# Weight sums of the next pair in another buffer, GpSimd operations in pieces, gate rows asked one item ahead, in one decoder layer

## The chip, the cores and the metric

The kernel runs on one core of a Trainium2 chip. The metric is the device time of one execution in microseconds (us), as the median of several executions. The engines are named as in the profile: PE is TensorE (PEld its weight loads), DVE is VectorE, ACT is ScalarE, POOL is GpSimd, SP is SyncE, which here issues most DMA transfers.

## The reference

One layer of a hybrid decoder on 1024 positions and 16 learned meta tokens (1040 rows of 1024 channels), all in float32: a short gated convolution and stick-breaking attention in parallel on one normalised input, merged by sigmoid gates, then a gated MLP with a causal convolution.

```python
def hybrid_mixer(xn, w_in, conv_w_mix, w_proj_conv, w_proj_attn, b_gate, w_out):
    h = xn @ w_in
    b_c, c_c, h_c, q, k, v, g_conv, g_attn = jnp.split(h, list(splits), axis=-1)
    y_conv = b_c * causal_dwconv(c_c * h_c, conv_w_mix)
    branch_conv = y_conv @ w_proj_conv
    o = stick_breaking_attention(q.reshape(hd), k.reshape(hd), v.reshape(hd))
    branch_attn = o.reshape(bsz, seq_len, D_ATTN) @ w_proj_attn
    merged = sigmoid(g_conv + b_gate[0]) * branch_conv + sigmoid(g_attn + b_gate[1]) * branch_attn
    return merged @ w_out

def conv_gated_mlp(xn, w_up_gate, conv_w_ffn, w_down):
    u, g = jnp.split(xn @ w_up_gate, 2, axis=-1)
    u = causal_dwconv(u, conv_w_ffn)
    return (jax.nn.gelu(u) * g) @ w_down
```

In the attention a weight is A[t,s] = sigmoid(z_ts) times the product over s < j < t of (1 - sigmoid(z_tj)), for s < t. Around each sub-layer stand RMS norms: x plus the norm of the mixer's result, and that plus the norm of the MLP's result.

## The kernel before

All products are made in a three-product form of reduced float32: each operand is split into a high part (a cast, `hi`) and a low part (the operand less its high part, `lo`), and PE adds hi x hi, hi x lo and lo x hi. `split(hi, lo, src, engine)` is that step: ACT casts (L64), then DVE or POOL subtracts (L65). The three matmul lines of a dense chunk are L128 to L130; the weights of a chunk are cast by ACT (L109) and split by POOL in four pieces (`wlo`, L112).

The work runs in stages. After the input norm (0 to 50 us) come the columns of `w_in` in chunks of 342 rows, interleaved with the attention (to about 1000 us): for each head and block of queries PE makes `z`, ACT the sigmoids, DVE scans from the right (`fl`, L340), POOL multiplies (`be`, L343) and cuts off the upper triangle (L344), and PE transposes the weights (L377), which DVE splits (`al`, L65). The helper around the kernel lays out the order of instructions on each engine by a planner, so a change of buffers or of code order can move rows elsewhere too.

Then, from about 1000 to 1220 us, the two branch projections follow, in items of 128 output channels. `item_pc(ob)` multiplies the convolution branch by its gate rows (`gcl`) and stores the product in `m_d`. `item_pa(ob)` loads the attention gate's rows (`gal`, L612) and the stored branch (`ml`, L613), DVE multiplies the projection by the gate (L615), POOL adds `ml` (L616) in three chunks, the first two query blocks are split into `mb`, and the rest goes to `mm_d` (L625). Between these items SP loads the rows of `w_out` (L640), ACT casts them and POOL splits them (`w_o`, L65). The loads share a few rotating buffers (`raw`, `gal`).

From 1220 to 1335 us nine row blocks of 114 rows go through the output projection. Each has two norms: the sum over the squares, `rstd_of` (L72 to L77, small DVE operations with a square root on ACT), the row plus the input (`row`, L732), its squares, a second `rstd_of`, and the normalised row `xv` (L738). `xvs` are two buffers for the input row and the normalised row, by turns, so the last block (8) uses `xvs[0]`. PE transposes `xv` (L745) into `xr`, and the operations `x_t1` to `x_t4` (L775) and `op_split` make from it the operands of a Strassen-Winograd product (`opB`, `opT`).

From 1335 to 1790 us 22 pairs of weight blocks are multiplied, seven products each (L863, L865, L867). `prep_pair` makes the seven weight operands of a pair: A11, S1, S2, A12, S3, S4, A22. S1 is the sum of two quarter blocks, made in `tmp_s` (L835), S2, S3 and S4 are differences in `raw` (L775), and `keep` splits each into an `a_op` buffer, cast on ACT and difference on POOL. When A22 is split, the next pair's load takes its `raw` buffer. ACT copies three partial results of a product to `snap` (L872, L875, L878). The pair's preparation runs while the pair before is multiplied, and pair 1's begins during the last row norms. The down projection fills the rest.

Of the kernel before, what the change touches and what calls it, by code (L numbers as in the profile page):

```python
# [11 lines left out]
ALU = mybir.AluOpType  # L12
# [20 lines left out]
def block_kernel(ctx, tc, x, meta_tokens, g_pre_mix, w_in, channels, w_proj_conv,  # L33
# [25 lines left out]
    act_d = tc.dram_tile([DFF, D], F32, name="act_d")  # L59
    h_d = tc.dram_tile([NQ, D], F32, name="h_d")  # L60


    def split(hi, lo, src, lo_engine=None):
        nc.scalar.copy(hi, src)  # L64
# [250 lines left out]
    def stage1(p, h, g):  # L315
# [3 lines left out]
        for b in range(3 * g, 3 * g + 3):  # L319
# [19 lines left out]
            def weights(fl=fl, be=be, nk=nk):  # L339
                nc.vector.tensor_tensor_scan(fl[:, :nk][:, ::-1], fl[:, :nk][:, ::-1],  # L340
                                             upper[:, NT - nk:][:, ::-1], 1.0,
                                             op0=ALU.mult, op1=ALU.max)
                nc.gpsimd.tensor_tensor(be[:, 0:nk - 1], be[:, 0:nk - 1], fl[:, 1:nk], op=ALU.mult)  # L343
                nc.gpsimd.affine_select(out=be[:, nk - QB:nk], in_=be[:, nk - QB:nk],  # L344
                                        pattern=[[-1, QB]], compare_op=ALU.is_gt, fill=0.0,
                                        base=0, channel_multiplier=1)
                pad = min(P * (-(-nk // P)), nk_end)
                if pad > nk:
                    nc.gpsimd.memset(be[:, nk:pad], 0.0)
# [229 lines left out]
    def src_of(tiles):  # L579
# [3 lines left out]
            return t[:, 0, kb, o:o + n], t[:, 1, kb, o:o + n]  # L583
        return src

    def item_pc(ob):
        st = {}

        def evac(ci, a, n, ps):
            if ci == 0:  # L590
                st["g"] = sw.tile([P, NT], F32, name="gcl", tag="wk")
                nc.sync.dma_start(st["g"][:, :NQ], gc_d[ob * P:(ob + 1) * P, :])
            g = st["g"]
            nc.vector.tensor_tensor(g[:, a:a + n], g[:, a:a + n], ps, op=ALU.mult)
            if ci == 2:
                nc.sync.dma_start(m_d[ob * P:(ob + 1) * P, :], g[:, :NQ])
        return (col_block(w_proj_conv, ob), src_of(yT), CH3, evac)
# [5 lines left out]
        return mb[b]  # L603

    def item_pa(ob):
        st = {}

        def evac(ci, a, n, ps):
            if ci == 0:
                st["g"] = sw.tile([P, NT], F32, name="gal", tag="wk")  # L610
                st["m"] = sw.tile([P, NT], F32, name="ml", tag="ld")
                nc.sync.dma_start(st["g"][:, :NQ], ga_d[ob * P:(ob + 1) * P, :])  # L612
                nc.sync.dma_start(st["m"][:, :NQ], m_d[ob * P:(ob + 1) * P, :])  # L613
            g, m = st["g"][:, a:a + n], st["m"][:, a:a + n]
            nc.vector.tensor_tensor(g, g, ps, op=ALU.mult)  # L615
            nc.gpsimd.tensor_tensor(g, g, m, op=ALU.add)  # L616
            if ci == 0:
                for b in range(2):
                    t = mb.get(b)
                    if t is None:  # L620
                        t = m_tile(b)
                    split(t[:, 0, ob, :], t[:, 1, ob, :], g[:, b * QB:(b + 1) * QB])
            if ci == 2:
                gv = st["g"][:, 2 * QB:NQ].rearrange("p (b n) -> p b n", n=QB)
                nc.sync.dma_start(mm_d[:, :, ob * QB:(ob + 1) * QB].rearrange("b p n -> p b n"), gv)  # L625
        return (col_block(w_proj_attn, ob), src_of(oT), CH3, evac)

# [62 lines left out]
    def load_m(b):  # L690
# [3 lines left out]
        raw = raw.rearrange("p (k n) -> p k n", k=KB)  # L694
        nc.sync.dma_start(raw, mm_d[b - 2].rearrange("p (k n) -> p k n", k=KB))
        t = m_tile(b)
        split(t[:, 0], t[:, 1], raw, nc.gpsimd if b > 5 else nc.vector)

    def out_products(b, c):
        n = min(CH, D - c * CH)  # L700
# [115 lines left out]
    def prep_pair(i):  # L816
# [7 lines left out]
        else:  # L824
            tmp_s = shared.get("tmp")
            if tmp_s is None:
                tmp_s = shared["tmp"] = mpool.tile([P, 512], F32, name="tmp_s", tag="mb")

        def keep(name, src):
            t = ring_tile()  # L830
            split(t[:, 0], t[:, 1], src, nc.gpsimd)
            got[name] = t

        keep("A11", a11)
# [400 lines left out]
```

## Time and profile before

| what | value |
|---|---|
| median of 3 runs | 2044.26 us (2043.37 to 2045.91) |
| profiled execution, its own time | 2045.85 us |
| its span | 2044.2 us |
| mean granted clock of PE | 0.993 |
| DMA | 177.58 MB, 87 GB/s on average |
| POOL instructions | 998 |

The span is the stretch that the trace covers, 1.65 us shorter than the execution. Durations of single instructions and waits come from this one execution. A row such as "PE tp L745 <- DVE xv L738" says that PE's `tp` instructions of line 745 waited for DVE's `xv` of line 738. The granted clock is PE's clock as a share of full speed.

### The profile page before, as it was taken

Reading aid. Unit: us, or ns where it says so; the run is one execution under the profiler, and the core shown is the slowest. Engines: PE = TensorE matmul, PEld = TensorE weight load, DVE = VectorE, ACT = ScalarE, POOL = GpSimd, SP = SyncE. Lnnn points to the kernel's source line nnn. Section 1 sums busy time; section 2 is a strip of 40 time slices with the busy share of each in tenths; the row PEclk is TensorE's granted clock in tenths of the full one; section 3 lists DMA queues with packets and bytes.
Section 4 is the critical chain, followed back from the end, with each engine's and each line's share of the span. In section 5 each row is a group of like instructions: output and inputs, shape, how many; then the busy total and the mean of one; then the engine's idle time right before and its main releaser. Section 6 shows DMA issues by size and latency. Waiting matters only on the chain.

```text
span 2044.2 us, 30953 instructions
## 1 busy us (share of the span) xinstructions
PE 1982.2 (97%) x12228; PEld 1857.7 (91%) x12228; DVE 1006.6 (49%) x1545; ACT 851.5 (42%) x1771; POOL 997.5 (49%) x998
## 2 busy tenths in 40 slices
PE   6999999999999999999999989979999999999997
PEld 6999999999999999999999989968998898878886
DVE  6545555555555555553341115784444434445546
ACT  5544555555554545554421113453344344421122
POOL 2543666465555646564223550336565555654353
PEclk9999999999999999999999999989999999999999
DMA  3111101111111111012574664313221212253223
GB/s 136 42 63 42 53 31 65 41 52 42 45 50 42 62 38 56 32 62 74 175 228 157 184 184 120 103 44 99 88 83 62 104 63 83 73 176 119 88 83 134
DMA packets 56174, 177.58 MB, mean 87 GB/s; under 512 B 12872, under 2 KB 12872, under 8 KB 56028
## 3 DMA queue, kind: packets, MB, share of 16 engines
q1 hardware_dynamic: 52704, 165.09, 24.9%
q10 hardware_dynamic: 3324, 10.50, 1.7%
q8 instruction: 96, 1.57, 0.3%
q14 instruction: 50, 0.41, 0.1%
HBM read 131.36 MB, written 44.21 MB: 86 GB/s over the span
## 4 chain that ended last, share of the span: by engine, by line
PE 79%; DVE 8%; DMA 6%; ACT 3%; POOL 2%; issue 2%; ACTq 0%; DVEq 0%; SPq 0%; POOLq 0%
PE mm L128 13%; PE mm L129 13%; PE mm L130 13%; PE st L863 6%; PE st L867 6%; PE st L865 6%; PE tp L377 3%; PE st L1155 3%; PE st L1157 3%; PE st L1156 3%; PE av L367 2%; PE av L368 2%; DMA xv<-in_x_dram 2%; PE z L331 2%; PE z L330 2%
## 5 line engine op out<-in xcount | busy, mean ns | idle before, releaser
L128 PE MATMUL mm<-xnT,whi 128*128 128x342 f32 (+2 forms) x1536 | 506.1, 330 | 0.3 <-ACT xnT L64 0.2
L129 PE MATMUL mm<-xnT,whi 128*128 128x342 f32 (+2 forms) x1536 | 493.5, 321 | 0.5 <-DVE xnT L65 0.5
L130 PE MATMUL mm<-xnT,wlo 128*128 128x342 f32 (+2 forms) x1536 | 492.0, 320 | 0.0
L112 POOL TENSOR_TENSOR wlo<-raw,whi 128x256 fp32r<-128x256 f32 x320 | 270.0, 876 | 208.0 <-ACT whi L109 207.9
L343 POOL TENSOR_TENSOR be<-be,fl 114x127 f32<-114x127 f32 (+2 forms) x144 | 181.0, 1257 | 284.0 <-DVE fl L340 268.0
L128 PEld LDWEIGHTS mm<-xnT,whi 128*128 128x128 f32 x1536 | 289.6, 189 | 5.0 <-ACT xnT L64 0.8
L129 PEld LDWEIGHTS mm<-xnT,whi 128*128 128x128 f32 x1536 | 290.2, 189 | 2.1 <-DVE xnT L65 1.0
L130 PEld LDWEIGHTS mm<-xnT,wlo 128*128 128x128 f32 x1536 | 289.7, 189 | 0.0
L340 DVE TENSOR_TENSOR_SCAN fl<-fl,upper 114x128 f32<-114x128 f32 (+2 forms) x144 | 215.6, 1499 | 117.0 <-ACT fl L332 103.0
L65 POOL TENSOR_TENSOR a_op<-raw,a_op 128x512 fp32r<-128x512 f32 (+1 forms) x136 | 191.2, 1419 | 91.4 <-ACT a_op L64 88.8
L65 DVE TENSOR_TENSOR al<-tp,ah 128x342 fp32r<-128x342 f32 (+4 forms) x288 | 127.1, 450 | 147.3 <-ACT ah L64 146.0
L64 ACT CAST ah<-tp 128x342 fp32r<-128x342 f32 (+4 forms) x288 | 112.8, 398 | 168.5 <-PE tp L377 160.2
L863 PE MATMUL st<-opT,a_op 128*128 128x258 f32 (+2 forms) x528 | 171.9, 326 | 4.7 <-ACT snap L878 1.6
L865 PE MATMUL st<-opT,a_op 128*128 128x258 f32 (+2 forms) x528 | 169.7, 321 | 2.9 <-DVE opT L65 2.0
L867 PE MATMUL st<-opT,a_op 128*128 128x258 f32 (+2 forms) x528 | 169.4, 321 | 0.0
L332 ACT ACTIVATE fl<-z 114x348 f32<-114x348 f32 (+10 forms) x240 | 111.5, 465 | 128.8 <-PE z L331 121.7
L64 ACT CAST a_op<-raw 128x512 fp32r<-128x512 f32 (+1 forms) x136 | 85.0, 634 | 154.7 <-DMA raw<-in_w_up_gate_dram 51.7
L1162 DVE TENSOR_TENSOR acc<-acc,st 128x512 f32<-128x512 f32 x144 | 98.5, 687 | 91.1 <-PE st L1157 91.1
L863 PE MATMUL st<-opB,a_op 128*128 128x512 f32 (+2 forms) x396 | 127.5, 322 | 0.0
L865 PE MATMUL st<-opB,a_op 128*128 128x512 f32 (+2 forms) x396 | 127.5, 322 | 0.0
L867 PE MATMUL st<-opB,a_op 128*128 128x512 f32 (+2 forms) x396 | 127.1, 321 | 0.0
L377 PE MATMUL tp<-ident,be 114*128 114x114 f32 x720 | 119.0, 263 | 6.8 <-DVE al L65 5.8
(169 smaller groups left out, 4314.0 us busy)
## 6 DMA issues: line engine op xcount, KB each, us to landing
raw<-in_w_in_dram SPq DMA_DIRECT2D x64, 512.0 KB, 3.4
raw<-in_w_up_gate_dram SPq DMA_DIRECT2D x44, 512.0 KB, 3.4
act_d<-owork SPq DMA_DIRECT2D x22, 512.0 KB, 4.3
araw<-act_d SPq DMA_DIRECT2D x22, 512.0 KB
raw<-in_w_down_dram SPq DMA_DIRECT2D x22, 512.0 KB, 3.4
y_d<-yy SPq DMA_DIRECT2D x8, 513.0 KB
ga_d<-gt SPq DMA_DIRECT2D x8, 513.0 KB
o_d<-ot SPq DMA_DIRECT2D x8, 513.0 KB
```

The source lines that it names most:

```text
L64: nc.scalar.copy(hi, src)
L65: (lo_engine or nc.vector).tensor_tensor(lo, src, hi.bitcast(F32), op=ALU.subtract)
L112: nc.gpsimd.tensor_tensor(lo[:, c], raw[:, c], hi[:, c].bitcast(F32), op=ALU.subtract)
L128: nc.tensor.matmul(ps, wh, xh, start=(kb == 0), stop=False)
L129: nc.tensor.matmul(ps, wh, xl, start=False, stop=False)
L130: nc.tensor.matmul(ps, wl, xh, start=False, stop=(kb == KB - 1))
L340: nc.vector.tensor_tensor_scan(fl[:, :nk][:, ::-1], fl[:, :nk][:, ::-1], upper[:, NT - nk:][:, ::-1], 1.0, op0=ALU.mult, op1=ALU.max)
L343: nc.gpsimd.tensor_tensor(be[:, 0:nk - 1], be[:, 0:nk - 1], fl[:, 1:nk], op=ALU.mult)
L377: nc.tensor.transpose(tp[:n, QB * j:QB * (j + 1)], blocks[j][0][:, kb * P:kb * P + n], ident[:QB, :QB])
L863: nc.tensor.matmul(ps, wt[:, 0, k], xh, start=start and kb == 0, stop=False, skip_group_check=True)
L865: nc.tensor.matmul(ps, wt[:, 0, k], xl, start=False, stop=False, skip_group_check=True)
L867: nc.tensor.matmul(ps, wt[:, 1, k], xh, start=False, stop=stop and kb == 3, skip_group_check=True)
```

## The change

There are three parts. The buffer `tmp_s` for the sums of pairs 1 and later is no longer a tile of the pool of `mb` but the first half of `xvs[0]`. POOL's operations are cut: the beta product (`be`) into pieces of at most 384 columns, the weight operands (`keep`, now by `pool_split`) into two of 256, the splits of the row blocks 6 to 8 (`mb`) into four of 228, the cast with them. And `fetch` asks for the gate rows of the next item (with `ml` in the attention projection) at the second chunk of the item before.

```diff
--- before.py
+++ after.py
@@ -59,6 +59,13 @@
     act_d = tc.dram_tile([DFF, D], F32, name="act_d")
     h_d = tc.dram_tile([NQ, D], F32, name="h_d")
 
+
+    def pool_split(hi, lo, src, pieces):
+        nc.scalar.copy(hi, src)
+        w = src.shape[-1] // pieces
+        for k in range(pieces):
+            c = slice(k * w, (k + 1) * w)
+            nc.gpsimd.tensor_tensor(lo[:, c], src[:, c], hi[:, c].bitcast(F32), op=ALU.subtract)
 
     def split(hi, lo, src, lo_engine=None):
         nc.scalar.copy(hi, src)
@@ -340,7 +347,11 @@
                 nc.vector.tensor_tensor_scan(fl[:, :nk][:, ::-1], fl[:, :nk][:, ::-1],
                                              upper[:, NT - nk:][:, ::-1], 1.0,
                                              op0=ALU.mult, op1=ALU.max)
-                nc.gpsimd.tensor_tensor(be[:, 0:nk - 1], be[:, 0:nk - 1], fl[:, 1:nk], op=ALU.mult)
+                w = -(-(nk - 1) // (-(-nk // 384)))
+                for a in range(0, nk - 1, w):
+                    e = min(a + w, nk - 1)
+                    nc.gpsimd.tensor_tensor(be[:, a:e], be[:, a:e], fl[:, a + 1:e + 1],
+                                            op=ALU.mult)
                 nc.gpsimd.affine_select(out=be[:, nk - QB:nk], in_=be[:, nk - QB:nk],
                                         pattern=[[-1, QB]], compare_op=ALU.is_gt, fill=0.0,
                                         base=0, channel_multiplier=1)
@@ -583,14 +594,25 @@
             return t[:, 0, kb, o:o + n], t[:, 1, kb, o:o + n]
         return src
 
+    fetched = {}
+
+    def fetch(kind, ob):
+        if ob > 7 or (kind, ob) in fetched:
+            return
+        g = sw.tile([P, NT], F32, name=f"g{kind}l", tag="wk")
+        nc.sync.dma_start(g[:, :NQ], (gc_d if kind == "c" else ga_d)[ob * P:(ob + 1) * P, :])
+        m = None
+        if kind == "a":
+            m = sw.tile([P, NT], F32, name="ml", tag="ld")
+            nc.sync.dma_start(m[:, :NQ], m_d[ob * P:(ob + 1) * P, :])
+        fetched[kind, ob] = (g, m)
+
     def item_pc(ob):
-        st = {}
-
         def evac(ci, a, n, ps):
-            if ci == 0:
-                st["g"] = sw.tile([P, NT], F32, name="gcl", tag="wk")
-                nc.sync.dma_start(st["g"][:, :NQ], gc_d[ob * P:(ob + 1) * P, :])
-            g = st["g"]
+            fetch("c", ob)
+            g = fetched["c", ob][0]
+            if ci == 1:
+                fetch("c", ob + 1)
             nc.vector.tensor_tensor(g[:, a:a + n], g[:, a:a + n], ps, op=ALU.mult)
             if ci == 2:
                 nc.sync.dma_start(m_d[ob * P:(ob + 1) * P, :], g[:, :NQ])
@@ -603,15 +625,12 @@
         return mb[b]
 
     def item_pa(ob):
-        st = {}
-
         def evac(ci, a, n, ps):
-            if ci == 0:
-                st["g"] = sw.tile([P, NT], F32, name="gal", tag="wk")
-                st["m"] = sw.tile([P, NT], F32, name="ml", tag="ld")
-                nc.sync.dma_start(st["g"][:, :NQ], ga_d[ob * P:(ob + 1) * P, :])
-                nc.sync.dma_start(st["m"][:, :NQ], m_d[ob * P:(ob + 1) * P, :])
-            g, m = st["g"][:, a:a + n], st["m"][:, a:a + n]
+            fetch("a", ob)
+            gt, mt = fetched["a", ob]
+            if ci == 1:
+                fetch("a", ob + 1)
+            g, m = gt[:, a:a + n], mt[:, a:a + n]
             nc.vector.tensor_tensor(g, g, ps, op=ALU.mult)
             nc.gpsimd.tensor_tensor(g, g, m, op=ALU.add)
             if ci == 0:
@@ -621,7 +640,7 @@
                         t = m_tile(b)
                     split(t[:, 0, ob, :], t[:, 1, ob, :], g[:, b * QB:(b + 1) * QB])
             if ci == 2:
-                gv = st["g"][:, 2 * QB:NQ].rearrange("p (b n) -> p b n", n=QB)
+                gv = gt[:, 2 * QB:NQ].rearrange("p (b n) -> p b n", n=QB)
                 nc.sync.dma_start(mm_d[:, :, ob * QB:(ob + 1) * QB].rearrange("b p n -> p b n"), gv)
         return (col_block(w_proj_attn, ob), src_of(oT), CH3, evac)
 
@@ -694,7 +713,11 @@
         raw = raw.rearrange("p (k n) -> p k n", k=KB)
         nc.sync.dma_start(raw, mm_d[b - 2].rearrange("p (k n) -> p k n", k=KB))
         t = m_tile(b)
-        split(t[:, 0], t[:, 1], raw, nc.gpsimd if b > 5 else nc.vector)
+        if b > 5:
+            for k in range(0, KB, 2):
+                split(t[:, 0, k:k + 2], t[:, 1, k:k + 2], raw[:, k:k + 2], nc.gpsimd)
+        else:
+            split(t[:, 0], t[:, 1], raw)
 
     def out_products(b, c):
         n = min(CH, D - c * CH)
@@ -824,11 +847,11 @@
         else:
             tmp_s = shared.get("tmp")
             if tmp_s is None:
-                tmp_s = shared["tmp"] = mpool.tile([P, 512], F32, name="tmp_s", tag="mb")
+                tmp_s = shared["tmp"] = xvs[0][:, :512]
 
         def keep(name, src):
             t = ring_tile()
-            split(t[:, 0], t[:, 1], src, nc.gpsimd)
+            pool_split(t[:, 0], t[:, 1], src, 2)
             got[name] = t
 
         keep("A11", a11)
```

What becomes of this in the order of instructions, at three places. First SP in the middle of the attention projection. The rows are the store of an item, the load of rows of `w_out` (into `raw`), the load of the stored branch (`ml`), of the attention gate's rows (`gal`) and of the next item's projection weights. Before:

```order
L625 DMA mm_d<-gal 128x7x114
L640 DMA raw<-in_w_out_dram 128x1024
L613 DMA ml<-m_d 128x1026
L612 DMA gal<-ga_d 128x1026
L100 DMA raw<-in_w_proj_attn_dram 128x1024
```

After:

```order
L644 DMA mm_d<-gal 128x7x114
L607 DMA ml<-m_d 128x1026
L659 DMA raw<-in_w_out_dram 128x1024
L603 DMA gal<-ga_d 128x1026
L107 DMA raw<-in_w_proj_attn_dram 128x1024
```

Only `ml` has moved, ahead of the load of `w_out`; `gal` keeps its place, and so do the gate rows `gcl` of the convolution projection.

Next POOL in the same stage: the additions of an item (`gal<-gal,ml`), the split of `w_out` (`w_o`) and of the next weights (`wlo`). Before:

```order
L65 TENSOR_TENSOR w_o<-raw,w_o 128x8x128
L616 TENSOR_TENSOR gal<-gal,ml 128x342 x2
L112 TENSOR_TENSOR wlo<-raw,whi 128x256 x4
L616 TENSOR_TENSOR gal<-gal,ml 128x342
L65 TENSOR_TENSOR w_o<-raw,w_o 128x8x128
```

After:

```order
L72 TENSOR_TENSOR w_o<-raw,w_o 128x8x128
L635 TENSOR_TENSOR gal<-gal,ml 128x342
L119 TENSOR_TENSOR wlo<-raw,whi 128x256 x4
L635 TENSOR_TENSOR gal<-gal,ml 128x342 x2
L72 TENSOR_TENSOR w_o<-raw,w_o 128x8x128
```

One addition has moved from behind the split of `w_out` to ahead of it.

Last DVE in the last row norm and behind it, up to the operands of pair 0 and the sums of pair 1. Before, the norm:

```order
L72 TENSOR_SCALAR v<-s_14221 114x1
L757 COPY xr<-tp 128x4x114
L74 RECIPROCAL s<-s 114x1
L835 TENSOR_TENSOR tmp_s<-raw 128x512
L75 SCALAR_TENSOR_TENSOR t<-s,v 114x1
L775 TENSOR_TENSOR raw<-raw 128x512
L76 TENSOR_SCALAR t<-t 114x1
L775 TENSOR_TENSOR raw<-tmp_s,raw 128x512
L77 TENSOR_TENSOR s<-s,t 114x1
L732 SCALAR_TENSOR_TENSOR row_13092<-row_13092,s,xv_13090 114x1024
L72 TENSOR_SCALAR v<-s_14235 114x1
L74 RECIPROCAL s<-s 114x1
```

After, the norm:

```order
L81 RECIPROCAL s<-s 114x1
L82 SCALAR_TENSOR_TENSOR t<-s,v 114x1
L83 TENSOR_SCALAR t<-t 114x1
L84 TENSOR_TENSOR s<-s,t 114x1
L755 SCALAR_TENSOR_TENSOR row_13236<-row_13236,s,xv_13234 114x1024
L79 TENSOR_SCALAR v<-s_14403 114x1
L81 RECIPROCAL s<-s 114x1
L82 SCALAR_TENSOR_TENSOR t<-s,v 114x1
L83 TENSOR_SCALAR t<-t 114x1
```

The operations `tmp_s<-raw`, `raw<-raw` and `raw<-tmp_s,raw` have left it. They now stand further on, after the norm's transposes, among the operands of pair 0 (`opB`, `opT`; `xv` is the buffer that took the place of `tmp_s`):

```order
L72 TENSOR_TENSOR opB_14380<-xr,opB_14380 128x4x256
L72 TENSOR_TENSOR opT_13225<-xr,opT_13225 128x4x115
L858 TENSOR_TENSOR xv_13234<-raw 128x512
L798 TENSOR_TENSOR xr<-xr 128x1024
L798 TENSOR_TENSOR raw<-raw 128x512
L798 TENSOR_TENSOR xr<-xr 128x1024
L72 TENSOR_TENSOR opT_14381<-xr,opT_14381 128x4x256
L798 TENSOR_TENSOR xr<-xr 128x1024
L72 TENSOR_TENSOR opT_14379<-xr,opT_14379 128x4x256
L941 TENSOR_TENSOR owork<-st,snap 128x255
L72 TENSOR_TENSOR opT_14470<-xr,opT_14470 128x4x256
L798 TENSOR_TENSOR raw<-xv_13234,raw 128x512
```

The last of the three stands behind the split of the last operand, `opT_14470`.

## The prediction

> **What bounds the kernel now.** I read the page's engine shares and chain first, then TensorE's waits, then the stretches in which those waits fall, then the timelines of the engines that end them. From the page:
>
> ```profile
> PE 1982.2 (97%) x12228; PEld 1857.7 (91%) x12228; DVE 1006.6 (49%) x1545; ACT 851.5 (42%) x1771; POOL 997.5 (49%) x998
> PE 79%; DVE 8%; DMA 6%; ACT 3%; POOL 2%; issue 2%; ACTq 0%; DVEq 0%; SPq 0%; POOLq 0%
> ```
>
> TensorE (PE) is busy 97% of the span and holds 79% of the chain that ends last; GpSimd (POOL) works 49%. An added POOL instruction therefore costs only where PE waits for what stands behind it, and the change can win no more than PE's waits and the slow clock that follows them. PE's waits in the whole program (us in all, times, longest one):
>
> ```profile
> PE tp L745 <- DVE xv L738: 7.6, 2, 6.8
> PE mm L128 <- DVE gal L615: 7.0, 1, 7.0
> PE tp L377 <- DVE al L65: 5.8, 8, 2.0
> PE st L865 <- DVE opT L65: 2.0, 2, 1.7
> PE st L863 <- ACT snap L878: 1.6, 2, 1.3
> ```
>
> The first, 6.8 of its 7.6 us in one piece, is the norm of the last row block; the second, one wait of 7.0 us, lies at the end of the attention projection; the third, eight waits of up to 2.0, is the attention's transposes; the last two are the operands and weight sums of the first pairs. The three parts of the change point at these rows. Around them the clock falls (length, busy PE, PEld, DVE, ACT, POOL with counts, then the granted clock, the DMA share, GB/s):
>
> ```profile
> 1205.65:1212.47 6.82, 4.25 (x15) 4.25 (x16) 1.73 (x5) 1.28 (x5) 5.18 (x6) 0.50 0.70 219
> 1335.00:1350.00 15.00, 8.05 (x46) 7.87 (x47) 12.02 (x25) 7.03 (x10) 1.24 (x1) 0.66 0.10 31
> 1350.00:1375.00 25.00, 21.30 (x120) 18.36 (x119) 23.30 (x19) 15.87 (x24) 12.48 (x8) 0.93 0.13 43
> ```
>
> At half clock the 4.25 us of work in the first row cost half of that, 2.1 us, beside the wait of 7.0 us. The waits and the slow clock of these rows are the largest that the change reaches, so the result is decided at about 1200 and between 1335 and 1380 us.
>
> **The change, step by step.** POOL's timeline in the middle of the attention projection and at its end serves two of the steps (start, length, line, tiles, count, and in brackets the wait before):
>
> ```profile
> 1154.60 2.22 POOL L65 TENSOR_TENSOR w_o<-raw,w_o 128x1024 fp32r<-128x1024 f32 x1 [6.68 <-ACT w_o L64]
> 1156.78 1.81 POOL L616 TENSOR_TENSOR gal<-gal,ml 128x342 f32<-128x342 f32 x2
> 1158.54 2.82 POOL L112 TENSOR_TENSOR wlo<-raw,whi 128x256 fp32r<-128x256 f32 x4
> ...
> 1168.84 2.21 POOL L65 TENSOR_TENSOR w_o<-raw,w_o 128x1024 fp32r<-128x1024 f32 x1 [6.59 <-ACT w_o L64]
> ...
> 1203.89 2.18 POOL L65 TENSOR_TENSOR w_o<-raw,w_o 128x1024 fp32r<-128x1024 f32 x1 [4.35 <-ACT w_o L64]
> 1206.02 0.91 POOL L616 TENSOR_TENSOR gal<-gal,ml 128x342 f32<-128x342 f32 x1
> ```
>
> *Pieces in stage 1.* POOL works off four tiles of 256 columns in 2.82 us and one of 1024 in 2.18 to 2.22, so a cut costs (2.82 - 2.18) / 3 = 0.21 us. The beta product (`be`) by shape, and POOL's wait for it:
>
> ```profile
> L343 POOL TENSOR_TENSOR be<-be,fl 114x1039 f32<-114x1039 f32 x16 | 32.5, 2030 | 4.4 <-DVE fl L340 3.9
> ```
>
> ```profile
> POOL be L343 <- DVE fl L340: 268.0, 64, 7.8
> ```
>
> The beta product of 1039 columns takes 2030 ns; in three pieces 2.03 + 2 x 0.21 = 2.45 us. The change adds 144 such instructions, 144 x 0.21 = 30 us of POOL, in stages where POOL sits idle 268.0 us before this very product: the idle time covers it. What can be won is a part of the 5.8 us in which PE waits for DVE's `al`, if DVE's scan no longer stands behind a whole product; the ends are -3 (half of the eight waits) and +1 (the affine select comes 0.42 us later in the long blocks, and one wait in three takes it over). I take -0.5, near zero, because the releaser is DVE's own split and not POOL.
>
> *Attention projection.* POOL's order changes: of an item's three additions (gate product plus convolution branch) one now stands behind the split of w_out (`w_o`), where two stood. SP's changes too: the branch rows `ml` are asked ahead of the w_out load. The gate rows `gal` keep their place behind it. SP's timeline in the middle of the stage, before the change:
>
> ```profile
> 1147.06 0.33 SPq L640 DMA_DIRECT2D raw<-in_w_out_dram  x1
> 1147.44 0.42 SPq L613 DMA_DIRECT2D ml<-m_d  x1
> 1152.74 0.32 SPq L612 DMA_DIRECT2D gal<-ga_d  x1
> ```
>
> POOL is in a ring here: the w_out split ends at 1156.82, two additions (1.8) and four splits of the next projection weights (2.8) follow, then the next w_out load is asked, lands, is cast and split. One addition fewer ahead of the weights shortens a turn by 0.9 us. Against that, `ml`, 128 x 1026 x 4 bytes, goes into the same queue ahead of w_out's 128 x 1024 x 4. How much it delays w_out no row shows. The lower end is nothing (w_out is asked 4 to 5 us after the store and `ml` may be through by then), the upper end is one whole transfer of that size, which these rows of the chain of waits give:
>
> ```profile
> 1152.74 3.49 DMA gal<-ga_d
> ...
> 1187.29 4.36 DMA raw<-in_w_out_dram
> ...
> 1195.02 7.72 DMA raw<-in_w_out_dram
> ...
> 1370.47 3.40 DMA raw<-in_w_up_gate_dram
> ```
>
> So a turn of 14.24 us (1154.60 to 1168.84) becomes 0.9 shorter to 2.6 longer (3.49 - 0.9). I take half a transfer less the addition, 1.75 - 0.9 = +0.85 us, for the turns in which both meet, and these are few, since POOL's ring only reaches PE at its end. There the order is unchanged: four splits, the w_out load (1195.02, landed 7.72 us later), the split at 1203.89, the addition at 1206.02, then this on VectorE (DVE):
>
> ```profile
> 1207.66 1.35 DVE L615 TENSOR_TENSOR gal<-gal,mm 128x342 f32<-128x342 f32 x3
> ```
>
> Nothing of that chain is taken out. The load took 7.72 us where the one before it took 4.36: with 4.36 again the chain ends 3.4 us sooner whatever the change does, with `ml` in its way it does not. Ends for this term: all of the wait and its slow clock down to the 2 us that the other stretches keep, (7.0 - 2) + 2.1 = -7; six turns at about +1 that reach PE, +6. I take -0.5: the end of the chain a little earlier by one addition, the transfer as long as it was.
>
> *The last row norm.* Three DVE operations of pair 1 (the sum `tmp_s` and two differences `raw`) leave the chain of the row norm; the DVE timeline has them in it:
>
> ```profile
> 1335.69 0.67 DVE L835 TENSOR_TENSOR tmp_s<-raw 128x512 f32<-128x512 f32 x1
> 1336.45 0.69 DVE L775 TENSOR_TENSOR raw<-raw 128x512 f32<-128x512 f32 x1
> 1337.25 0.69 DVE L775 TENSOR_TENSOR raw<-tmp_s,raw 128x512 f32<-128x512 f32 x1
> 1338.05 1.28 DVE L732 SCALAR_TENSOR_TENSOR row<-row,s,xv 114x1024 f32<-114x1024 f32 x1
> ...
> 1362.78 1.21 DVE L65 TENSOR_TENSOR opT<-xr,opT 128x1024 fp32r<-128x1024 f32 x1
> ...
> 1373.90 0.69 DVE L835 TENSOR_TENSOR tmp_s<-raw 128x512 f32<-128x512 f32 x1 [1.05 <-DMA raw<-in_w_up_gate_dram]
> 1374.68 1.70 DVE L775 TENSOR_TENSOR raw<-raw 128x512 f32<-128x512 f32 x1
> 1376.48 1.61 DVE L775 TENSOR_TENSOR raw<-tmp_s,raw 128x512 f32<-128x512 f32 x1
> ```
>
> Each puts off the next link of the norm by about 0.6 us less what the small operations hide of one another; they take 0.67 + 0.69 + 0.69 = 2.05, of which I count 1.6 (lower end 1.2, upper end 2.05). In rows 5 to 7 the product with the gain (`row<-po`) moves ahead of one operation on the transposed rows; that can bring the later row norms forward by nothing or by one such operation (1.28 from the row above is the nearest of that size); I take 1.0. So this term is -2.6, and the last opT split (1362.78) comes that much earlier, at about 1360.2, ending 1361.4.
>
> *Pair 1's sums, now behind that split.* The three operations do not vanish. The S2 difference now stands behind the last opT split, so its cast and its split on POOL start at 1361.4 + 0.69 = 1362.1 or later. POOL and ScalarE (ACT) at this place:
>
> ```profile
> 1366.65 3.80 POOL L65 TENSOR_TENSOR a_op<-raw,a_op 128x512 fp32r<-128x512 f32 x2 [1.52 <-ACT a_op L64]
> ```
>
> ```profile
> 1378.65 0.58 ACT L878 COPY snap<-st 128x512 f32<-128x512 f32 x1
> ```
>
> Behind S2 on POOL come S3, S4 and A22. One a_op split took 1.90 us here (3.80 for two), and a cut adds 0.21: four times 2.11 is 8.4, so A22 is done at 1362.1 + 0.6 for S2's cast + 8.4 = 1371.1, where the load of pair 2 that waits for it was asked at 1370.47. That load (3.40 us) leads to pair 2's three sums (from 1373.90), to the cast of its S2, and behind that cast stands ACT's copy `snap` (1378.65), for which PE waits (the row of L863 among its waits). So PE, which comes 2.6 us sooner, waits 1.3 + 2.6 us and more at that copy: the whole gain is given back. What softens it are the two differences at 1374.68 and 1376.48, 1.70 and 1.61 us beside running POOL splits where they take 0.69 alone: shorter pieces let them start earlier, by up to 2 x 0.95 = 1.9 us. The ends: 0 (A22 2 us earlier and both differences short) and +5 (A22 1.5 us later, the clock halved once more). I take +2.6, exactly what the norm won.
>
> The clock belongs to this term. The row of 1350 to 1375 us shows 0.93, that is (1 - 0.93) x 25 / 0.5 = 3.5 us at half clock, though PE's longest wait there is the 1.7 us of L865. So short waits already cost a slow stretch here, and the new, longer wait takes the place of one rather than adding one: 0. The Trainium skill ("TensorE: Matmul & The Clock Gate", Part 1) puts the halving after an idle window of some 3.4 us; by that rule the present stretch would have no slow clock and the new wait of 4 us would bring one, an estimate of +1.7 us and a sum of +0.2 in place of -1.5. The 0.93 does not agree with it as it stands.
>
> *Pieces in the products.* 22 pairs x 7 splits = 154 cuts at 0.21 us, 32 us of POOL. DVE waits for these splits, DVE's differences are long beside them, and PE waits little (the third fence, 1400 to 1800 us, where products and their sums meet):
>
> ```profile
> DVE raw L775 <- POOL a_op L65: 106.6, 20, 7.6
> ```
>
> ```profile
> L775 DVE TENSOR_TENSOR raw<-raw 128x512 f32<-128x512 f32 x39 | 48.7, 1249 | 107.5 <-POOL a_op L65 106.6
> ```
>
> ```profile
> PE st L863 <- ACT snap L872: 0.6, 2, 0.4
> PE st L863 <- DVE owork L918: 0.6, 1, 0.6
> ```
>
> The differences take 1249 ns on average where 0.69 is the bare time, and DVE idles 106.6 us before them; but PE's own two waits there are 1.2 together. The ends are -1.2 and +1 (32 us more on an engine which half the time waits for something else); I take -0.5. The nine cuts of the `mb` splits lie before the rows that need them and are in the -2.6.
>
> The sum: -0.5 - 0.5 - 2.6 + 2.6 - 0.5 = -1.5 us against the profiled execution, whose own time was 2045.85 (span 2044.2 and 1.65 around it): 2044.35. That execution stood 1.59 over the median of the runs shown, 2044.26, so the forecast for the median is 2042.8. What a measurement of this kernel can tell from no change is about 0.2%, 4.1 us: I forecast no difference.
>
> **The rivals.** *Faster: POOL's ring opens.* If `ml` has landed before w_out is asked, each turn is 0.9 us shorter, the last load is asked sooner and takes 4.36 as the one before it; the split ends 3.4 + 0.9 earlier, PE's wait falls from 7.0 to under 3, its slow clock goes, -7 as above, with half of the row norm's gain kept: -8.5, some 2036. For it: the shorter order, and that 4.36 was the usual length. Against it: the last turn's order is the same. *Slower: `ml` ahead of w_out.* At each turn w_out lands later by what of `ml` is still under way. It decides from 0.9 us on, where the addition saved is used up; at one whole transfer, 3.49, a turn is 2.6 longer. PE needs this only as far as its lead over POOL is used up, which at 1200 it is: three turns at 2.2 give +6.5, some 2051. For it: the last load shows that the queue can take 7.72, and PE has no lead left at 1200. Against it: `ml` in the second place had been in the queue as well, right behind. *Slower too: the wait at the copy grows.* If the eight pieces behind S2 meet the 128 x 1024 operations of DVE one after the other, A22 ends 3 us later than reckoned, PE waits near 7 us at the copy and some 2 us of slow clock follow: 5 more than forecast, 2047.8. *The change does not do what it says:* the gate rows `gal` still stand behind w_out and still wait for a buffer, so only `ml` moves, by one place; then the second term is 0 and the time 2043.3, inside the forecast.
>
> **How the numbers follow.** The forecast, with the rival that nothing moves, 0.43, by itself 2040.2 to 2047.5; the open ring 0.34, 2033 to 2040; `ml` in the way 0.17 and the grown wait 0.06, 2047.5 to 2053. The forecast and the nearer halves of both sides make 2034 to 2051, outside which the rest of about 0.2 lies. Faster by more than 0.2%: 0.34; within: 0.43; slower: 0.23.
>
> **What would show it.** The first step is right if the waits of L377's counterpart stay between 3 and 6 us. The second: SP's timeline shows w_out landing later after its issue or not, and TensorE's wait for `gal` near 1200 is again 5 to 8 us (the open ring: under 3). The third: no sum of pair 1 between the links of the norm, and the wait for `xv` near 5 instead of 6.8 us. The fourth: PE's wait for the third `snap` near 1376 grows from 1.3 to 3 to 6 us, and the load of pair 2 is asked at 1370 to 1372. The fifth: the differences at 0.7 to 1.0 us on average, with no change of PE's time from 1400 to 1790. The prediction is wrong first of all if the transfers in the projection stage fall out otherwise than before, and next if pair 2's load comes as early as the row norm gained.

## The result and the profile after

The changed kernel takes 2074.35 us (median of 4 runs, 2072.27 to 2078.19) against 2044.57 for the kernel before: the ratio is 1.0154, with a 95% interval from 1.0138 to 1.0169. It is 1.5%, some 30 us, slower, where no difference was forecast.

The engines' shares on the page of the changed kernel:

```profile
PE 1992.7 (96%) x12228; PEld 1864.7 (90%) x12228; DVE 997.5 (48%) x1545; ACT 852.9 (41%) x1780; POOL 1066.1 (51%) x1305
```

POOL has 307 instructions and 68.6 us more than before (1066.1 against 997.5); the prediction's count of cuts, 0.21 us each, gave 64. The loss does not lie in that sum but in where PE waits and in the slow clock behind some of these waits. PE's waits in the whole changed kernel (us in all, times, longest):

```profile
PE st L886 <- ACT snap L895: 16.4, 9, 1.9
...
PE st L886 <- ACT snap L901: 7.1, 2, 6.1
PE tp L768 <- DVE xv L761: 5.4, 2, 5.2
PE st L886 <- DVE owork L941: 5.1, 8, 1.0
PE mm L135 <- DVE gal L634: 4.8, 3, 3.8
PE tp L388 <- DVE al L72: 4.5, 8, 2.1
```

Three of the waits of before have shrunk: `xv` from 6.8 to 5.2 us at the longest, and in all `gal` from 7.0 to 4.8 and `al` from 5.8 to 4.5. For `xv` and `al` that holds in every profiled kernel of this document with the same part of the change. For `gal` it does not: in the nine kernels with the old loads of the gate rows the wait is 2.6 to 7.0 us, in the seven with the new ones 4.3 to 8.7. Two rows are new in size. The copy of L901 (L878 before), behind pair 2's casts, grew from 1.6 to 7.1. And the first copy of a product, L895 (L872 before), now holds PE nine times for 16.4 us, 1.7 to 1.9 each; before it had 0.6 in the products. Where these lie, by the same stretch of the products in both kernels, first before and then after (length, busy PE, PEld, DVE, ACT, POOL, then clock, DMA share, GB/s):

```profile
1400.00:1800.00 400.00, 396.98 (x2461) 354.06 (x2460) 178.78 (x216) 166.49 (x285) 228.98 (x167) 1.00 0.24 85
```

```profile
1400.00:1800.00 400.00, 380.20 (x2366) 340.42 (x2366) 162.72 (x203) 157.03 (x274) 244.75 (x291) 0.99 0.22 72
```

PE is idle 3 us of 400 before and 20 after, at a clock of 1.00 and 0.99. If the n-th matmul of one trace is held against the n-th of the other, the changed kernel is 0.1 us ahead at 1180 us of before, 0.8 ahead at 1213 and 5.5 ahead at 1364; between 1374 and 1387 it loses 7.0; from 1394, where it is 1.7 behind, to 1773 it falls back evenly to 28.9 behind; to the end nothing more happens (29.0). So some 27 us were lost, nearly evenly, over the products of pairs 2 to 21, a stretch to which the prediction had given -0.5. Over the same matmuls, again before and after:

```profile
1394.04:1790.08 396.04, 394.52 (x2476) 353.52 (x2474) 176.55 (x214) 164.95 (x283) 225.89 (x166) 1.00 0.23 80
```

```profile
1395.70:1819.13 423.43, 402.89 (x2475) 359.07 (x2474) 175.19 (x216) 165.01 (x283) 257.38 (x298) 0.99 0.23 74
```

Of the 27.4 us, 19.0 are idle time of PE (20.5 us against 1.5). The other 8.4 are longer work of PE (402.9 against 394.5); three stretches of 3.4 us at half clock account for 5.1 of these, and the rest is not explained here.

**How the even loss comes about.** In every second pair POOL also multiplies three results (`owork<-owork,snap`) between the weight splits of the next pair. POOL's timeline there, before:

```profile
1418.77 3.80 POOL L65 TENSOR_TENSOR a_op<-raw,a_op 128x512 fp32r<-128x512 f32 x3 [2.08 <-ACT a_op L64]
1423.80 1.31 POOL L931 TENSOR_TENSOR owork<-owork,snap 128x512 f32<-128x512 f32 x1 [1.23 <-DVE snap L930]
1425.07 1.30 POOL L65 TENSOR_TENSOR a_op<-raw,a_op 128x512 fp32r<-128x512 f32 x1
1426.33 1.30 POOL L931 TENSOR_TENSOR owork<-owork,snap 128x512 f32<-128x512 f32 x1
1427.59 1.29 POOL L65 TENSOR_TENSOR a_op<-raw,a_op 128x512 fp32r<-128x512 f32 x1
1428.84 1.31 POOL L931 TENSOR_TENSOR owork<-owork,snap 128x512 f32<-128x512 f32 x1
1430.48 1.29 POOL L65 TENSOR_TENSOR a_op<-raw,a_op 128x512 fp32r<-128x512 f32 x1 [0.33 <-ACT a_op L64]
```

and after:

```profile
1421.71 3.53 POOL L68 TENSOR_TENSOR a_op<-raw,a_op 128x256 fp32r<-128x256 f32 x5 [1.28 <-ACT a_op L64]
1426.48 1.31 POOL L954 TENSOR_TENSOR owork<-owork,snap 128x512 f32<-128x512 f32 x1 [1.23 <-DVE snap L953]
1427.75 1.44 POOL L68 TENSOR_TENSOR a_op<-raw,a_op 128x256 fp32r<-128x256 f32 x2
1429.14 1.31 POOL L954 TENSOR_TENSOR owork<-owork,snap 128x512 f32<-128x512 f32 x1
1430.41 1.44 POOL L68 TENSOR_TENSOR a_op<-raw,a_op 128x256 fp32r<-128x256 f32 x2
1431.82 1.31 POOL L954 TENSOR_TENSOR owork<-owork,snap 128x512 f32<-128x512 f32 x1
1433.09 0.73 POOL L68 TENSOR_TENSOR a_op<-raw,a_op 128x256 fp32r<-128x256 f32 x1
```

Before, three whole splits stand ahead of the first multiplication (S2, A12, S3), S4 ahead of the second, A22 ahead of the third. After, there are five pieces ahead of the first, and between the multiplications two pieces each time, which are no longer one operand: S3's second with S4's first, then S4's second with A22's first, and A22's second behind the third. Counted from the first instruction behind the first multiplication (1425.07 before, 1427.75 after), S4 is done 1.3 us later in the kernel before and 3.4 us later in the changed one, A22 3.8 and 6.1 us later. Each of the two is the last reader of a buffer into which half of the next pair's weights are loaded. SP's issue of the first of these loads, before and after:

```profile
1426.39 0.33 SPq L813 DMA_DIRECT2D raw<-in_w_up_gate_dram  x1
```

```profile
1431.18 0.33 SPq L836 DMA_DIRECT2D raw<-in_w_up_gate_dram  x1
```

It goes out at the end of S4's split in both. (The second load waits for A22's split.) ACT then waits for it, with the cast of the next pair's A11, and the copy on which PE depends stands behind that cast. ACT before, ACT after, and PE after:

```profile
1429.78 0.62 ACT L64 CAST a_op<-raw 128x512 fp32r<-128x512 f32 x1 [3.98 <-DMA raw<-in_w_up_gate_dram]
1430.31 0.37 ACT L872 COPY snap<-st 128x258 f32<-128x258 f32 x1
```

```profile
1434.59 0.62 ACT L64 CAST a_op<-raw 128x512 fp32r<-128x512 f32 x1 [5.57 <-DMA raw<-in_w_up_gate_dram]
1435.11 0.37 ACT L895 COPY snap<-st 128x258 f32<-128x258 f32 x1
```

```profile
1435.53 0.39 PE L886 MATMUL st<-opT,a_op 128*128 128x258 f32 x1 [1.82 <-ACT snap L895]
```

Before, the copy is done at 1430.68 and the same matmul starts at 1430.73 without a wait; after, PE waits 1.82 us in the shown place (2.1 from the start of one matmul to the start of the next). Since the next loads wait for the next splits, the delay comes again in every second pair.

### The profile page after: what moved, and what is told of

Its sections match the earlier page's. It is cut to its first block, busy times and chain, and to the rows that moved or that the text cites. A ratio compares the mean times of both kernels' runs of the same rounds, so it can differ in the third digit from the quotient of the medians.

```text
span 2072.7 us, 31226 instructions
## 1 busy us (share of the span) xinstructions
PE 1992.7 (96%) x12228; PEld 1864.7 (90%) x12228; DVE 997.5 (48%) x1545; ACT 852.9 (41%) x1780; POOL 1066.1 (51%) x1305
## 3 DMA queue, kind: packets, MB, share of 16 engines
q1 hardware_dynamic: 52704, 165.09, 24.9%
## 5 line engine op out<-in xcount | busy, mean ns | idle before, releaser
L353 POOL TENSOR_TENSOR be<-be,fl 114x271 f32<-114x271 f32 (+14 forms) x288 | 206.0, 736 | 261.7 <-DVE fl L347 254.2
L68 POOL TENSOR_TENSOR a_op<-raw,a_op 128x256 fp32r<-128x256 f32 x264 | 214.2, 837 | 68.3 <-ACT a_op L64 65.0
L886 PE MATMUL st<-opT,a_op 128*128 128x258 f32 (+2 forms) x528 | 174.5, 330 | 28.6 <-ACT snap L895 16.4
L64 ACT CAST a_op<-raw 128x512 fp32r<-128x512 f32 x132 | 80.9, 621 | 175.4 <-DMA raw<-in_w_up_gate_dram 75.8
L886 PEld LDWEIGHTS st<-opT,a_op 128*128 128x128 f32 x528 | 101.0, 191 | 44.6 <-ACT snap L895 18.5
L888 PE MATMUL st<-opB,a_op 128*128 128x512 f32 (+2 forms) x396 | 129.1, 326 | 2.0 <-DVE opB L72 1.9
L886 PE MATMUL st<-opB,a_op 128*128 128x512 f32 (+2 forms) x396 | 129.0, 326 | 0.0
L890 PE MATMUL st<-opB,a_op 128*128 128x512 f32 (+2 forms) x396 | 128.5, 324 | 0.0
```

Source lines behind the costliest of these rows:

```text
L68: nc.gpsimd.tensor_tensor(lo[:, c], src[:, c], hi[:, c].bitcast(F32), op=ALU.subtract)
L353: nc.gpsimd.tensor_tensor(be[:, a:e], be[:, a:e], fl[:, a + 1:e + 1], op=ALU.mult)
L886: nc.tensor.matmul(ps, wt[:, 0, k], xh, start=start and kb == 0, stop=False, skip_group_check=True)
L888: nc.tensor.matmul(ps, wt[:, 0, k], xl, start=False, stop=False, skip_group_check=True)
L890: nc.tensor.matmul(ps, wt[:, 1, k], xh, start=False, stop=stop and kb == 3, skip_group_check=True)
```

## The experiments

Theory A is this one: the place of the second pieces of S4 and A22 costs the time. Theory B gives it to the cuts' own price, theory C to the other parts of the change. Each run was timed beside the kernel before, whose median was 2042.7 to 2046.4 us in these sessions; ratios and differences are to the kernel before in the same session, while the expected times were reckoned from about 2044. Where a stretch of a trace is given, it comes from one profiled execution of each kernel.

**Whole operands, cuts alone, cuts in the old order, whole operands in a late place.** The first changes one line of the changed kernel, as shown; the second puts the cut operands alone into the kernel before:

```diff
-            pool_split(t[:, 0], t[:, 1], src, 2)
+            split(t[:, 0], t[:, 1], src, nc.gpsimd)
```

> The changed kernel with the weight operands split whole again (128x512), all else as changed. Theory A (the place): cut in two, the second pieces of S3, S4 and A22 stand one multiplication `owork<-owork,snap` later on POOL, so the buffers of the next pair's weights come free 2.1 us later, ACT's cast of A11 waits for them, and the copy `snap` behind it holds PE 2 us in every second pair; whole operands restore the order, so the time falls by about 28 us to 2042 to 2048. Theory B (the price): each cut costs 0.21 us on POOL, 1.5 us a pair, and that lengthens every pair; the same fall. Theory C (the other parts: the sums in xvs[0], the beta pieces, the fetch): the time stays at 2070 to 2078.

> The kernel before with the weight operands cut in two and nothing else. Theories A and B: 2069 to 2077, PE's wait of 2 us for the first snap copy in every second pair. Theory C: 2042 to 2047.

Measured: whole operands 2047.79 us, ratio to before 1.0007 (0.9995 to 1.0018); cuts alone 2074.04 us, 1.0136 (1.0119 to 1.0154). The cut of the weight operands is the whole loss, and the other parts together win nothing that can be told. Theory C falls; A and B are not told apart.

The third keeps all cuts and binds POOL's order, for which it also starts the preparation of a pair two steps earlier; the fourth cuts nothing and binds S4 and A22 behind one more multiplication (the main lines of both edits):

```diff
+ # third, on the changed kernel: each multiplication behind the last piece placed before it
+                with tc.issue_after(last_cut[0].ins):
+                    nc.gpsimd.tensor_tensor(v, v, s, op=ALU.mult)
+ # fourth, on the kernel before
+            if name in ("S4", "A22") and i > 1 and i % 2 == 0:
+                with tc.issue_after(mults[-2 if name == "S4" else -1].ins):
+                    split(t[:, 0], t[:, 1], src, nc.gpsimd)
```

> The changed kernel with all its cuts, but POOL's order bound so that both pieces of S3 stand ahead of the first multiplication, both of S4 ahead of the second and both of A22 ahead of the third, as the whole ones did before. Theory A: S4 is done 0.14 us later than whole and A22 0.28, so most of the 28 us comes back: 2043 to 2050, the wait for the first snap copy under 0.5 us. Theory B: the cuts are all there, so 2068 to 2076.

> The kernel before, no cut anywhere, but in every second pair S4's split is put behind the second multiplication on POOL and A22's behind the third: each 1.31 us later. Theory A: the first load of the next pair comes 1.3 us later, less some 0.25 us of slack, ten times: 2052 to 2058, with PE waits of about 1 us at the first snap copy. Theory B: no cut, no cost, 2042 to 2047.

Measured: cuts in order 2050.32 us, 1.0019 (1.0008 to 1.0029); late whole operands 2064.95 us, 1.0090 (1.0073 to 1.0108), 18.6 us over before. Theory B is refuted twice: with all 154 cuts the loss is 4 us, and with none at all it is 18.6. (The third alone would not do it, as the earlier preparation is a second difference.) The late place's price was larger than the 8 to 14 expected. PE's waits in the third and in the fourth kernel:

```profile
PE st L889 <- ACT snap L904: 10.8, 11, 6.4
```

```profile
PE st L867 <- ACT snap L876: 15.6, 10, 3.1
...
PE st L867 <- DVE owork L922: 4.6, 8, 1.2
```

The fourth has the waits of the changed kernel without a cut: the first copy (L876) ten times, and a second kind, for DVE's `owork`. In the third the first copy's row has shrunk to a single wait of 0.8 us; the 10.8 us at the third copy (L904) are 6.4 once at pair 2, 1.0 once before it and, over the products, nine short waits of 0.4 at most, where ACT now has two casts ahead of that copy instead of one.

**ACT's cast behind the copy.** The changed kernel, with A11's cast bound behind the latest copy:

```diff
+            if i > 1 and name == "A11":
+                with tc.issue_after(last_snap[0].ins):
+                    pool_split(t[:, 0], t[:, 1], src, 2)
```

> The changed kernel, all cuts and POOL's order as in it, but ACT's cast of A11 is bound behind the latest `snap` copy, so that the late load of the next pair no longer stands between PE and that copy. Theory A, by this path (late split, late load, ACT's cast waits, the copy behind it waits, PE waits): the ten waits of 2.1 us for the first copy go, the smaller ones by way of DVE's first sum, which waits for the second load, stay: 2052 to 2058. Rival A2, PE waits for the operands themselves and ACT's queue is not the path: 2069 to 2077, the wait only under another name.

Measured 2083.89 us, 1.0201 (1.0181 to 1.0221): worse than the changed kernel, and outside both expected ranges. My path by ACT alone was too narrow. The rival was right in that the wait came back under another name, but PE did not wait for the operands themselves. Two of PE's waits, and DVE around one of the first kind:

```profile
PE st L892 <- DVE owork L947: 23.1, 11, 2.7
...
PE st L892 <- ACT snap L907: 9.2, 11, 5.5
```

```profile
1434.89 0.69 DVE L864 TENSOR_TENSOR xv<-raw 128x512 f32<-128x512 f32 x1 [7.02 <-DMA raw<-in_w_up_gate_dram]
1435.78 0.69 DVE L798 TENSOR_TENSOR raw<-raw 128x512 f32<-128x512 f32 x1 [0.20 <-DVE xv L864]
1436.61 0.69 DVE L798 TENSOR_TENSOR raw<-xv,raw 128x512 f32<-128x512 f32 x1
1437.22 1.09 DVE L947 TENSOR_TENSOR owork<-st,snap 128x258 f32<-128x258 f32 x3
```

DVE waits 7.02 us for the second load with its sum (L864), and the additions of results (L947), which PE needs, stand behind it. The late loads thus reach PE through two queues; with one of them opened PE waits in the other. That the round from split to load to split sets the pace is my reading of it. In the products PE was idle for 24.9 us (20.5 in the changed kernel) and at half clock for 27 us (10), so the clock has a large part in the loss.

**Which load, and how many cuts.** S4 and A22 whole in the changed kernel (five of seven cuts stay), and only these two cut in the kernel before (the one line that decides, of each):

```diff
+ pool_split(t[:, 0], t[:, 1], src, 1 if name in ("S4", "A22") else 2)   # on the changed kernel
+ pool_split(t[:, 0], t[:, 1], src, 2 if name in ("S4", "A22") else 1)   # on the kernel before
```

> The changed kernel with S4 and A22 split whole and the other five operands still cut: five of the seven cuts remain. Only the second piece of S3 still stands behind the first multiplication, so S4 and A22 are done some 0.7 us later than before, not 2.1 and 2.2. Theory A, by the place, with what the run of late whole operands cost (18.6 us for 1.3 us): 2049 to 2056. A price by the number of cuts, 5/7 of 28 us: 2062 to 2067.

> The kernel before with only S4 and A22 cut in two: two of the seven cuts. Their second pieces stand one multiplication later, S4 done 1.45 us later than before and A22 1.65. Theory A: about 20 us slower than before, 2060 to 2068. A price by the number of cuts, 2/7 of 28 us: 2049 to 2054.

Measured 2050.98 us, 1.0023 (1.0010 to 1.0035), and 2068.74 us, 1.0101 (1.0072 to 1.0130). Five cuts cost some 5 us, and two cuts some 22 (0.7 above the expected range): it depends on which operands are cut. The two alone bring the whole wait: in the products PE was idle 19.3 us with them and 18.2 with all seven operands of a pair cut. The loss there was 21.6 and 27.4, and five stretches of 3.4 us at half clock with all cut, none with two, make 8.5 us: in the profiled executions the clock accounts for the difference, not the other five cuts. The last run keeps S4 in its old place and binds only A22's split behind the third multiplication:

> The kernel before, no cut, S4 in its old place and only A22's split put behind the third multiplication in every second pair: only the second load of the next pair is late, by 1.3 us. If the period is set by the first load (A11's cast and the copy behind it on ACT): 2042 to 2048, no difference from before. If by the second as well (the sum on DVE, and the additions of results behind it): 2052 to 2062, with PE's waits for DVE's `owork`.

Measured 2052.17 us, 1.0038 (1.0023 to 1.0053), 7.8 us, at the lower end of what was expected for the second load. PE's wait there:

```profile
PE st L867 <- DVE owork L922: 8.1, 11, 2.0
```

The second load alone makes PE wait for DVE, eleven times. If the two effects add, the other 10.8 of the 18.6 us with both late belong to the first load, within the 8 to 14 expected of its path; that is not shown, since no run has S4 alone late.

**The other parts alone.** The sums in `xvs[0]`, the fetch, and the cut beta products and row blocks, each alone on the kernel before:

> The kernel before with tmp_s in xvs[0] and nothing else. By the prediction's third and fourth step the wait for xv falls from 6.8 to about 5 us and PE's wait at the third copy of pair 1 grows from 1.3 to 4 us or more; together -1 to +3: 2043 to 2049. Rival, the gain is kept: 2040 to 2043.

> The kernel before with the fetch one item ahead and nothing else. By the prediction's second step the time stays within 3 us of before, with a wait of 4 to 8 us for gal near 1200. Rival open ring: under 2040. Rival `ml` in the way: over 2050.

> The kernel before with the beta product and the row blocks' splits in pieces, nothing else. By the prediction's first step: the transposes' waits of 5.8 us become 4 to 5, 31 us more of POOL's time without effect, 2040 to 2044. Rival, the pieces slow DVE's scans: 2046 to 2050.

Measured: sums 2045.13 us, 1.0008 (0.9999 to 1.0018); fetch 2044.19 us, 1.0008 (0.9998 to 1.0018); beta and row blocks 2041.17 us, 0.9973 (0.9960 to 0.9986). PE's waits with the sums alone, and with the cut beta products and rows:

```profile
PE tp L745 <- DVE xv L738: 5.2, 1, 5.2
PE st L863 <- ACT snap L878: 3.6, 2, 2.6
```

```profile
PE tp L381 <- DVE al L65: 4.1, 7, 2.1
```

The sums shorten the norm's wait to 5.2, as the third step said, and lengthen the copy's (1.6 to 3.6), as the fourth said, though its longest wait is 2.6 where 4 or more were expected. The pieces of the beta product and the rows are the part of the change that pays, 5.5 us. PE's wait for `al` falls by 1.7 (5.8 to 4.1), and this is no accident of one execution: it is 3.8 to 4.8 us in the eight profiled kernels with cut beta products and 5.8 to 7.7 in the eight without. At 1000 us of before, the eight with them are 0.7 to 2.9 us ahead of the profile of before, the seven others between 1.2 ahead and 2.5 behind, on average nearly 3 us apart. Between 1282 and 1329 us, among the row blocks, this run wins another 2.1 us, but five kernels that leave the rows whole win as much there (cuts alone, sums alone, casts behind the copies, the last two cut, A22 late): the profile of before has waits of 0.9 and 0.8 us in that place that most others have not. A gain from the rows' pieces is therefore not shown. The profiled execution ended 3.9 us earlier than that of before; the rest of the 5.5 it does not show.

**A faster version.** Every cast of pair 2 and later bound behind the copies (the same lines, `if i > 1:` for all names), with whole operands in the changed kernel, then alone on the kernel before, then with the cut beta products and rows and nothing else of the change:

> The run with whole operands, and every cast of an operand of pair 2 and later bound behind the latest `snap` copy on ACT. If the 4.6 us that PE lost at 1377 us (the third copy behind pair 2's casts) was only this order, the row norm's gain stays and the time is 2040 to 2044. Rival: pair 1's or pair 2's operands are late themselves and PE waits for them instead: 2045 to 2049.

> The kernel before with every cast of an operand of pair 2 and later bound behind the latest `snap` copy on ACT, nothing else. If the 5 us of the version with whole operands and this order come from the row norm's gain that is kept only with it, this alone gives 0 to -2: 2041 to 2044. If they come from ACT's order alone: 2036 to 2039.

> The kernel before with the casts of the operands behind the `snap` copies and with the beta and row block splits in pieces, weight operands whole, sums and fetch as before. Alone these gave 6.5 and 5.5 us. If they add: 2032 to 2036. If they are partly the same gain: 2037 to 2040.

Measured 2037.45 us, 0.9976 (0.9965 to 0.9987); 2039.89 us, 0.9968 (0.9956 to 0.9980); 2036.40 us, 0.9964 (0.9950 to 0.9978). All three beat both kernels. The first is faster than either range expected for it (2040 to 2044, 2045 to 2049). In the second the order of casts wins 6.5 us on the kernel before, so it does not need the norm's gain: that was the second of the two cases named, whose range it missed by 0.9. In the products PE then has a single wait, of 0.7 us, and none at all in the first and the last. The last is the fastest by its median and falls between its two ranges: it wins 7.4 us where the two gains alone would add up to 12. So they seem to be partly the same, though the intervals of the three runs just leave room for the sum.

## Why the prediction was wrong

The step that failed is the fifth, *Pieces in the products*, with -0.5 between -1.2 and +1. It measured +27 to +28: 19 us of new idle time of PE, 5 at half clock and the rest unexplained. I priced the cuts by their own time, 32 us, and set against it that POOL has idle time and that PE waited little; that is right for an engine's load and says nothing on its order. The sign it named came nearly as said (DVE's differences fell to 1.07 us, 0.7 to 1.0 expected), and PE's time rose all the same. The order of the changed kernel's POOL in the products (five pieces, a multiplication, two, a multiplication, two, a multiplication, one) was not read. And the loads were left out of the step: which split frees the buffer that a load waits for, and that this load had no slack (the copy on ACT was done 0.05 us before PE went on). The range was too narrow by the same omission, since neither rival for a slower result had this place.

*Stage 1*, -0.5: the waits for `al` fell to 4.5, as forecast (3 to 6), but the term was set too small. Alone, with the rows' pieces, the part gave 5.5 us (0.27%, interval 0.14 to 0.40%), and the traces show nearly 3 of them by the end of this stage.

*Attention projection*, -0.5: right. The fetch alone made no difference. At 1213 us the changed kernel was 0.6 further ahead than at 1180; neither `ml` in the way nor the open ring came. PE's wait near 1200 was shorter than the 5 to 8 us said (3.8), but four shorter ones, 0.3 to 0.9 us and 2.2 in all, stood ahead of it.

*The last row norm*, -2.6: right. The wait for `xv` became 5.2 ("near 5"; it is 5.2 in all seven kernels with the moved sums and 6.8 in the nine others), and between 1329 and 1364 us the changed kernel won 3.4, the six others with the moved sums 2.7 to 3.0 (those without at most 1.4, but the cuts alone 2.8). That the pieces of the rows have a share in it, as the prediction put it, no run shows.

*Pair 1's sums*, +2.6: the mechanism was right, the size was not. A22 was done at 1370.4 (1371.1 said), but the load behind it took 4.7 us instead of 3.4, and PE waited 6.1 us at the copy where 3 to 6 were expected; 7.0 us were lost between 1374 and 1387. The sums alone lost 4.6 us between 1364 and 1394, the changed kernel 7.2. The clock took part, which I had set to 0. The stretches of after:

```profile
1350.00:1372.00 22.00, 20.05 (x109) 17.35 (x109) 17.37 (x16) 13.28 (x18) 14.43 (x12) 0.93 0.08 26
1375.00:1400.00 25.00, 20.15 (x114) 17.85 (x115) 9.37 (x14) 5.65 (x11) 14.07 (x17) 0.86 0.38 123
```

Before, the stretch of the second row was at 1.00; now it is at 0.86, which is (1 - 0.86) x 25 / 0.5 = 7 us at half clock, beginning within the wait of 6.1. The Trainium skill ("TensorE: Matmul & The Clock Gate", Part 1) lets the clock fall after an idle window of some 3.4 us. The wait of 6.1 us agrees. The nine waits for the first copy in the products, of 1.7 to 1.9 us, do not agree throughout: three of them were each followed by 3.4 us at half clock. The 3.4 us around the first of these waits and the 3.4 us behind them:

```profile
1475.92:1479.33 3.41, 1.67 (x14) 1.45 (x14) 0.00 (x0) 1.17 (x3) 1.96 (x4) 1.00 0.99 309
1479.33:1482.74 3.41, 3.41 (x19) 3.41 (x18) 0.69 (x1) 0.38 (x1) 0.33 (x1) 0.50 0.72 257
```

At the other two, PE was busy for 1.63 and 1.55 us of the 3.4 ahead. The slow clock in the row that begins at 1350 is of the same kind: all of it lies before 1353, behind a wait of 1.9 us for `opB` that ended at 1348.6. So the prediction read the row of before rightly: short waits already cost a slow stretch. That the new wait would add nothing was wrong by little: between 1335 and 1400 us PE was at half clock for 17.1 us instead of 13.7, which costs 1.7. The slow stretches in the products stood in none of its terms.

## What to carry to other kernels

An instruction cut in two takes two places in its engine's queue, and whatever the scheduler puts between them delays what the whole one released. Before cutting, look at which instruction frees a buffer for the next load, and read the new order at that place, however idle the engine is; cut the operations that release nothing, and leave the last readers of a buffer whole. Where an engine's order has an instruction that waits for a load ahead of one for which the busiest engine waits, try to exchange the two: with whole operands and all casts that won 5 to 7 us on the kernel before, but with A11's cast alone in the changed kernel the wait moved to another engine and the time rose.

## What the runs showed of the hardware

A cut is cheap on POOL itself: two pieces of 128x256 took 1.44 us where a whole 128x512 took 1.30, 0.14 us a cut, in both kernels with a DVE operation beside it that takes one input from `st`. DVE's differences beside the cut splits took less, as this row shows for 1378 to 1790 us of the changed kernel (1249 ns before):

```profile
L798 DVE TENSOR_TENSOR raw<-raw 128x512 f32<-128x512 f32 x38 | 40.8, 1073 | 108.2 <-POOL a_op L68 106.2 <-DVE xv L858 2.0
```

That is in line with the Trainium skill ("SBUF — State Buffer", Who interferes with whom), by which a DVE operation with two inputs in SBUF contends with a POOL instruction that reads SBUF, for ports that are locked exclusively. The 0.18 us won on each did not show in the time: the same cuts alone made the kernel 28 us slower.
